# Three small moves inside the mixers of a hybrid decoder: a bank, a granule, and rows dealt 5 and 3

## The chip, the core and the metric

The kernel runs on one core of a Trainium2 chip. The metric is the device time of one execution in microseconds. Engines are named as in the profile: PE is TensorE (PEld its weight loads), DVE VectorE, ACT ScalarE, POOL GpSimd, SP SyncE, which issues most DMAs. Each engine works through its own list of instructions in order, and semaphores hold an instruction until what it needs is there.

## What is computed

Two decoder layers on x of 512 tokens by 1024 features, float32. Each layer is a half-step SwiGLU, three token mixers side by side, and a second half-step SwiGLU:

```
for l in range(2):
    x = x + 0.5 * swiglu(rms_norm(x, ffn1_norm[l]), ffn1_w_in[l], ffn1_w_out[l])
    h = rms_norm(x, mix_norm[l]) @ w_mix_in[l]
    c_x, c_b, c_c, h_q, h_f, h_i, h_g, f_q, f_k, f_v, f_f = split(h)
    y = concat(short_conv(c_x, c_b, c_c),        # 256 channels: rows 0 and 1 of 128
               hgrn2(h_q, h_f, h_i, h_g),        # 4 heads of 64: rows 2 and 3
               fox(f_q, f_k, f_v, f_f))          # 8 heads of 64: rows 4 to 7
    x = x + y @ w_mix_out[l]                     # 1024 x 1024
    x = x + 0.5 * swiglu(rms_norm(x, ffn2_norm[l]), ffn2_w_in[l], ffn2_w_out[l])
```

The convolution is causal, three taps wide, and gated before and after. HGRN2 is a linear recurrence with per-channel decay, done in chunks of 64 tokens. Fox is causal softmax attention with normalised q and k and a forget gate: the logit of query t and key s gets c[t] - c[s], where c is the running sum over tokens of the log of a sigmoid of the gate f_f.

## The kernel before

Activations lie transposed, features on the 128 partitions and tokens in the free dimension. For accuracy each float32 operand is split in a high and a low part (fp32r), and a product is three matmuls: high by high (L316), high by low (L322), low by high (L323), all in `mm3`. A 512-column matmul is the unit of the projections.

Weights come in **granules** (`granule`, L280): one or more DMAs on SP's queue bring up to two blocks of 128 rows into a staging buffer `st` (two buffers); an ACT cast (L305) writes the high part into a buffer `hl` (three buffers), and a DVE subtraction (L306) the low part. A granule of 256 columns in two row blocks feeds 12 matmuls of 512 columns into two banks. `stream_steps` (L331) yields after each granule, so that other work can be put in between.

PSUM has eight banks, which `bank` (L248) hands out under four names: `mm` three, `sc` two, `pt` two, `po` one. `sc` is used for attention scores and some of HGRN2, `pt` for transposes, `po` for the attention's output, `mm` for projections. A bank is free for the next taker of its name when the last reader of its previous content is through. `next4` (L251) takes either `sc`, `sc`, `pt`, `pt` or `mm`, `mm`, `mm`, `po`.

The code is a Python program that gives out instructions; the framework then orders each engine's list, by the order in which instructions are given out as a priority, and by when it reckons their operands and buffers ready. An instruction given out later can thus stand earlier on its engine, if the one before it is reckoned not ready.

The mixer (`mix`, L997) goes in this order:

1. Projections for HGRN2, values together with the fox gates (into `mm`, `sc`, `sc`, `mm`).
2. HGRN2 (`hgrn`, L1237), with the fox projections of q, k and v put between its steps. Beside its first two steps run the two parts of `fox_decay` (L1461): first the log of the gates, split in `flh` and `fll` (L1471, L1472); then their running sum over tokens, eight small matmuls against a triangle of ones (L1477) into one bank `cb` (L1474, a `pt` bank), from which ACT and DVE make `negc` (L1482, L1483). The step of HGRN2 given out just before transposes two blocks into the two `pt` banks (L1284), from which ACT copies them (L1287).
3. Attention, heads 0 to 3 (`fox_attend`, L1549). Each of 16 turns stands for one head and 128 queries: scores run three turns ahead (L1558, L1559 into `sc`), a softmax on DVE and ACT (L1563 to L1571), transposes of the probabilities P into `pt` (L1623), their split (L1625, L1626), and with each second turn the products with V (L1581 into `po`). After each head the two halves of the `po` bank are added (L1594, L1595), and after each second head the row of 128 features is split (L1598, L1599; tiles `fyh`, `fyl`). `beside` (L1158) puts the convolution's twelve granules (`conv`, L1145) between the turns, one per turn from n = 2 on, with n counted from `first`. At n = 3 the function `finish` gives out the rest of HGRN2, which reads two `pt` banks (L1442 and L1445).
4. Attention, heads 4 to 7, with most of the out-projection beside it (`most`, L1181): four groups of 256 output columns, each into two `mm` banks, each over the first rows of `order` (L1168). Rows 2 and 3 are HGRN2 (tile `hy`), 0 and 1 the convolution (`cyh`, `cyl`), 4 and 5 heads 0 to 3, 6 and 7 heads 4 to 7.
5. The remaining rows of the out-projection, in two groups of 512 columns, each into four banks of `next4`. Each bank is added to x (L1179), and the pieces of the next norm are made from it (`norm_part`). The second FFN follows.

Of the kernel before, what the change touches and what calls it, by code (L numbers as in the profile page):

```python
# [156 lines left out]
class Trunk:  # L157
# [109 lines left out]
    def act(self, out, in_, func, **kw):  # L267
        i = self.nc.scalar.activation(out, in_, func, **kw)
        if self.tab is not None:
            self.tc.add_manual_dep(i.ins, self.tab, NOSYNC, reason="table order")  # L270
        self.tab_users.append(i.ins.name)
        return i
# [724 lines left out]
    def mix(self, l, w, w_out, conv_w, out_gain, q_gain, k_gain, f_bias, next_gain):  # L997
# [3 lines left out]
        with tc.tile_pool(name=self.n("mix"), bufs=1) as mp:  # L1001
# [103 lines left out]
            def projections():  # L1105
                for hf in range(2):
                    yield from self.fox_qkv(mp, hf, tokens, half)

            dense = projections()
# [46 lines left out]
                    self.conv_out(ap2, i, bb[i])  # L1156

            def beside(attend, dense, first=0, then=()):  # L1158
                for n, _ in enumerate(attend, first):
                    if n == 3 and then:  # L1160
                        then()
                    if n >= 2:
                        next(dense, None)
                for _ in dense:
                    pass

            self.begin_norm(next_gain)
            order = [2, 3, 4, 5, 0, 1, 6, 7]  # L1168

            def rows(k0, a, n):  # L1170
                return lambda k, kk: [
                    w_out[order[k0 + k] * P : (order[k0 + k] + kk) * P, a : a + n]
                ]

            def act(k0):
                return lambda k: (self.yh[order[k0 + k]], self.yl[order[k0 + k]])

            def add(j, bank):
                nc.vector.tensor_add(self.xT[:, j, :], bank, self.xT[:, j, :])  # L1179

            def most():  # L1181
                for dg in range(4):
                    banks = [self.bank("mm") for _ in range(2)]
                    yield from self.stream_steps(
                        [(bk, c, None) for bk, c in zip(banks, FM2)],
                        rows(0, 256 * dg, 256), act(0), 6,
                    )
                    for i in range(2):
                        add(2 * dg + i, banks[i])

            beside(attend, conv(), 1, finish)
            beside(self.fox_attend(ap1, 1, half[1], qkg, {}), most())
            self.ntog = 0
            for dg in range(2):
                banks = self.next4()
                self.stream(
                    [(bk, c, None) for bk, c in zip(banks, TOK)],
                    rows(6, 512 * dg, 512), act(6), 2,
                )
                for i in range(4):  # L1200
                    j = 4 * dg + i
                    add(j, banks[i])
                    self.norm_part(j, ap2)
# [257 lines left out]
    def fox_decay(self, mp, zf):  # L1461
        nc = self.nc
        a = mp.tile([P, 4, NH], F32, tag="fa", name=self.n("fa"))
        lf = mp.tile([P, 4, NH], F32, tag="fl", name=self.n("fl"))
        nc.vector.scalar_tensor_tensor(out=a, in0=zf, scalar=-1.0, in1=zf, op0=ALU.mult, op1=ALU.min)
        self.act(a, a, AF.Exp)
        self.act(a, a, AF.Ln, bias=1.0)
        nc.vector.scalar_tensor_tensor(out=lf, in0=zf, scalar=0.0, in1=a, op0=ALU.min, op1=ALU.subtract)
        lh = mp.tile([P, 4, NH], F32R, tag="flh", name=self.n("flh"))
        ll = mp.tile([P, 4, NH], F32R, tag="fll", name=self.n("fll"))  # L1470
        nc.scalar.copy(lh, lf)  # L1471
        nc.vector.tensor_sub(ll, lf, lh)  # L1472
        yield
        cb = self.bank("pt")  # L1474
        for j in range(4):
            for part in (lh, ll):
                nc.tensor.matmul(  # L1477
                    cb[:NH, j * P :], part[:, j, :], self.utri[:, : T - j * P],
                    start=j == 0 and part is lh, stop=j == 3 and part is ll,
                )  # L1480
        self.negc = mp.tile([NH, 2, T], F32R, tag="negc", name=self.n("negc"))
        nc.scalar.activation(self.negc[:, 0, :], cb[:NH, :], AF.Copy, scale=-1.0)  # L1482
        nc.vector.scalar_tensor_tensor(  # L1483
            out=self.negc[:, 1, :], in0=cb[:NH, :], scalar=-1.0, in1=self.negc[:, 0, :],
            op0=ALU.mult, op1=ALU.subtract,
        )
# [338 lines left out]
```

## Time and profile before

| | us |
|---|---|
| median of 3 runs | 1816.66 (1815.56 to 1819.09) |
| the profiled execution | 1815.31 |
| its span, first to last instruction | 1813.2 |
| PE busy | 1801.3 (99%) |
| DVE busy | 1461.3 (81%) |
| ACT busy | 1001.0 (55%) |

One execution was profiled; its times are counted from its first instruction. The mixers lie at about 320 to 584 us and 1216 to 1480 us, the rest is FFNs. A line of a timeline has the start, the duration, engine, source line, operation, output and inputs by the program's names (buffer numbers left out), shapes and count; in brackets stands the time that the engine was idle before it, and what ended the wait. Matmuls overlap in a pipeline, so their rate is read from the distance of their starts, not from their duration. A line of the table of groups has, after the count, busy time and mean duration in ns, and then the idle time before them. A line of the table of stages has the stretch, its length, and busy time with the number of instructions for each engine.

### The profile page before, as it was taken

The numbers are of one execution on the slowest core, as the hardware profiler recorded it, in microseconds if no ns is written. First come the engines' busy times: TensorE is split into PE (matmuls) and PEld (weight loads), VectorE is DVE, ScalarE is ACT, GpSimd is POOL, SyncE is SP. The second block draws the span as 40 slices with busy tenths as digits, with TensorE's granted clock in tenths as the row PEclk, the third lists the DMA queues.
The fourth block names the chain that finished last, engine by engine and source line by source line (L and its number), as shares of the span: only waits on it lengthen the run. The fifth ranks groups of instructions, "written<-read, shape, count | busy, mean of one in ns | idle before, by whom it ended". The sixth has DMA issues, their size and how long they took to land.

```text
span 1813.2 us, 34777 instructions
## 1 busy us (share of the span) xinstructions
PE 1801.3 (99%) x14281; PEld 1682.8 (93%) x14281; DVE 1461.3 (81%) x2048; ACT 1001.0 (55%) x1434; POOL 170.3 (9%) x172
## 2 busy tenths in 40 slices
PE   9999999999999999999999999999999999999999
PEld 7899999899878899999889999998998788999997
DVE  9889787676887898889678887976868878888883
ACT  5455555464775565555445555555547755555551
POOL 0011120100000001112001111201000000020210
PEclk9999999999999999999999999999999999999999
DMA  6768783233323757868275787823233237687762
GB/s 197 186 135 191 179 175 96 74 79 85 87 82 105 216 136 161 197 159 168 82 207 130 163 193 192 163 68 79 77 90 86 82 102 212 163 158 192 158 134 93
DMA packets 243934, 250.94 MB, mean 138 GB/s; under 512 B 18456, under 2 KB 229152, under 8 KB 243776
## 3 DMA queue, kind: packets, MB, share of 16 engines
q1 hardware_dynamic: 189872, 182.38, 33.3%
q0 software_dynamic: 53600, 66.09, 22.8%
q8 instruction: 112, 1.84, 0.4%
q14 instruction: 46, 0.38, 0.1%
q10 hardware_dynamic: 304, 0.27, 0.0%
HBM read 223.98 MB, written 2.10 MB: 125 GB/s over the span
## 4 chain that ended last, share of the span: by engine, by line
PE 91%; DVE 5%; ACT 3%; issue 1%; DMA 0%; SPq 0%; ACTq 0%; DVEq 0%
PE mm L316 13%; PE mm L323 13%; PE mm L322 13%; PE sc L323 6%; PE sc L316 6%; PE sc L322 6%; PE pt L316 6%; PE pt L322 6%; PE pt L323 6%; PE po L316 4%; PE po L322 4%; PE po L323 4%; PE po L1581 1%; PE pt L1623 1%; ACT hl L305 1%
## 5 line engine op out<-in xcount | busy, mean ns | idle before, releaser
L784 ACT CAST hl<-w 128x1024 fp32r<-128x1024 f32 x322 | 337.1, 1049 | 318.2 <-PE mm L323 78.1
L786 DVE TENSOR_TENSOR hl<-w,hl 128x1024 fp32r<-128x1024 f32 x322 | 392.6, 1222 | 85.4 <-ACT hl L784 85.3
L306 DVE TENSOR_TENSOR hl<-st,hl 128x512 fp32r<-128x512 f32 (+2 forms) x188 | 161.6, 860 | 100.7 <-ACT hl L305 99.8
L305 ACT CAST hl<-st 128x512 fp32r<-128x512 f32 (+2 forms) x188 | 141.8, 754 | 176.8 <-PE po L323 62.3
L316 PE MATMUL mm<-xc,hl 128*128 128x256 f32 (+1 forms) x732 | 201.6, 276 | 0.5 <-ACT g L895 0.5
L323 PE MATMUL mm<-xc,hl 128*128 128x256 f32 x728 | 201.4, 277 | 0.0
L322 PE MATMUL mm<-xc,hl 128*128 128x256 f32 x728 | 201.4, 277 | 0.0
L323 PE MATMUL sc<-xc,hl 128*128 128x256 f32 x528 | 146.3, 277 | 0.0
L316 PE MATMUL sc<-xc,hl 128*128 128x256 f32 (+1 forms) x530 | 146.3, 277 | 0.0
L322 PE MATMUL sc<-xc,hl 128*128 128x256 f32 x528 | 146.2, 277 | 0.0
L316 PEld LDWEIGHTS mm<-xc,hl 128*128 128x128 f32 x732 | 137.4, 188 | 0.9 <-ACT g L895 0.7
L323 PEld LDWEIGHTS mm<-xc,hl 128*128 128x128 f32 x728 | 136.7, 188 | 0.1
L322 PEld LDWEIGHTS mm<-xc,hl 128*128 128x128 f32 x728 | 136.7, 188 | 0.0
L322 PE MATMUL pt<-xc,hl 128*128 128x256 f32 x480 | 133.0, 277 | 0.0
L316 PE MATMUL pt<-xc,hl 128*128 128x256 f32 (+1 forms) x484 | 133.0, 276 | 0.0
L323 PE MATMUL pt<-xc,hl 128*128 128x256 f32 x480 | 132.8, 277 | 0.0
L316 PE MATMUL mm<-x,hl 128*128 128x512 f32 x272 | 107.4, 395 | 0.0
L323 PE MATMUL mm<-x,hl 128*128 128x512 f32 x272 | 106.5, 392 | 0.4 <-DVE hl L306 0.4
L322 PE MATMUL mm<-x,hl 128*128 128x512 f32 x272 | 106.4, 391 | 0.0
L316 PEld LDWEIGHTS sc<-xc,hl 128*128 128x128 f32 x530 | 99.6, 188 | 0.2
L323 PEld LDWEIGHTS sc<-xc,hl 128*128 128x128 f32 x528 | 99.3, 188 | 0.1
L322 PEld LDWEIGHTS sc<-xc,hl 128*128 128x128 f32 x528 | 99.1, 188 | 0.0
(514 smaller groups left out, 5604.9 us busy)
## 6 DMA issues: line engine op xcount, KB each, us to landing
w<-in_ffn_w_in_dram SPq DMA_DIRECT2D x140, 512.0 KB
w<-in_ffn_w_out_dram SPq DMA_DIRECT2D x64, 512.0 KB
w<-in_ffn_w_out_dram POOLq DMA_DIRECT2D x56, 512.0 KB, 9.0
st<-in_w_mix_in_dram SPq DMA_DIRECT2D x88, 256.0 KB
st<-in_ffn_w_in_dram SPq DMA_DIRECT2D x70, 256.0 KB
w<-in_ffn_w_in_dram POOLq DMA_DIRECT2D x35, 512.0 KB, 8.2
w<-S POOLq DMA_DIRECT2D x35, 512.0 KB, 4.7
st<-in_ffn_w_out_dram SPq DMA_DIRECT2D x24, 512.0 KB
```

The source lines that it names most:

```text
L305: a = nc.scalar.copy(hi, src[:, c : c + w])
L306: b = nc.vector.tensor_sub(lo, src[:, c : c + w], hi)
L316: i = nc.tensor.matmul(acc[:, c], ah, bh[:, c], start=first and c.start == 0, stop=False, skip_group_check=True,)
L322: nc.tensor.matmul(acc, ah, bl, start=False, stop=False, skip_group_check=True)
L323: i = nc.tensor.matmul(acc, al, bh, start=False, stop=last, skip_group_check=True)
L784: A(nc.scalar.copy(hi, src))
L786: return lambda: V(nc.vector.tensor_sub(lo, src, hi))
L1581: nc.tensor.matmul(self.ob[:, t0 + u * P : t0 + 2 * P], V[:, j, h % 4].rearrange("p a d -> p (a d)"), part[:, j, u:, :].rearrange("p i t - ...
L1623: nc.tensor.transpose(tb[:, j * P : (j + 1) * P], p[:, j * P : (j + 1) * P], self.ident)
```

## The change

Three edits, none of which changes what is computed.

The fox gates' sums go into an `sc` bank instead of a `pt` bank. `beside` takes `first` granules of the dense work before the first turn that it drives; it is 1 for the convolution and 0 for the out-projection, so the convolution's granules each come one turn earlier. In the out-projection the rows' order becomes 2, 3, 0, 1, 4, 5, 6, 7, and five rows instead of six run beside the second half of the attention (granules of two, two and one row), which leaves three instead of two for the end (a granule of two rows, 5 and 6, and a granule of one row, 7, in each group).

```diff
             def beside(attend, dense, first=0, then=()):
+                for _ in range(first):
+                    next(dense, None)
                 for n, _ in enumerate(attend, first):
...
-            order = [2, 3, 4, 5, 0, 1, 6, 7]
+            order = [2, 3, 0, 1, 4, 5, 6, 7]
...
                         [(bk, c, None) for bk, c in zip(banks, FM2)],
-                        rows(0, 256 * dg, 256), act(0), 6,
+                        rows(0, 256 * dg, 256), act(0), 5,
...
                     [(bk, c, None) for bk, c in zip(banks, TOK)],
-                    rows(6, 512 * dg, 512), act(6), 2,
+                    rows(5, 512 * dg, 512), act(5), 3,
...
-        cb = self.bank("pt")
+        cb = self.bank("sc")
         for j in range(4):
```

## The prediction

> **What bounds the kernel now.** I read the page first, then busy time by stage, then the timeline of TensorE (PE) wherever two matmuls start further apart than their size needs.
>
> ```profile
> span 1813.2 us, 34777 instructions
> PE 1801.3 (99%) x14281; PEld 1682.8 (93%) x14281; DVE 1461.3 (81%) x2048; ACT 1001.0 (55%) x1434; POOL 170.3 (9%) x172
> PE 91%; DVE 5%; ACT 3%; issue 1%; DMA 0%; SPq 0%; ACTq 0%; DVEq 0%
> ```
>
> PE is the bound: 99% busy, 91% of the chain that ended last. No edit takes a matmul away, so the time can fall only by stalls of PE that vanish. By stage (columns: window, its length, then busy time of PE, PEld, DVE, ACT, POOL, then the granted clock):
>
> ```profile
> 470.00:518.00 48.00, 46.76 (x246) 38.23 (x246) 43.05 (x100) 36.75 (x83) 1.56 (x3) 1.00 0.29 78
> 518.00:566.00 48.00, 47.56 (x256) 38.32 (x255) 38.56 (x98) 35.08 (x81) 1.04 (x2) 1.00 0.32 91
> 566.00:584.00 18.00, 17.75 (x90) 14.03 (x89) 12.46 (x21) 9.83 (x18) 0.00 (x0) 1.00 0.26 83
> 584.00:1212.00 628.00, 628.00 (x4947) 605.27 (x4946) 521.80 (x577) 338.40 (x394) 75.84 (x64) 1.00 0.68 162
> 1364.00:1414.00 50.00, 48.83 (x257) 39.95 (x256) 43.61 (x101) 38.75 (x89) 2.08 (x4) 1.00 0.29 78
> ```
>
> The FFNs in the middle row idle 0.00 of 628 us. The attention half beside the convolution (first row) idles 1.24, the half beside the out-projection (second) 0.44, the mixer's tail (third) 0.25; the second layer's like half (last row) 1.17. The clock is 1.00 everywhere. So the stake is small: a few stalls per layer, each found twice.
>
> **Edit 1, the bank of the gates' sums.** Around L1477, from a timeline of all engines, then PE alone in layer 2:
>
> ```profile
> 388.32 0.19 DVE L1472 TENSOR_TENSOR fll<-fl,flh 128x32 fp32r<-128x32 f32 x1 [0.28 <-ACT flh L1471]
> 388.44 0.28 PE L322 MATMUL mm<-hl,x 128*128 128x256 f32 x1
> 388.56 0.28 PE L323 MATMUL mm<-hl,x 128*128 128x256 f32 x1
> 388.72 1.07 ACT L1287 COPY T<-pt 128x512 f32<-128x512 f32 x2
> 389.35 0.39 PE L1477 MATMUL pt<-utri,flh 128*8 128x512 f32 x1 [0.51 <-ACT T L1287]
> 391.72 0.67 DVE L1483 SCALAR_TENSOR_TENSOR negc<-pt,negc 8x512 fp32r<-8x512 f32 x1
> ```
> ```profile
> 1284.20 0.28 PE L323 MATMUL mm<-hl,x 128*128 128x256 f32 x1
> 1284.92 0.40 PE L1477 MATMUL pt<-utri,flh 128*8 128x512 f32 x1 [0.44 <-ACT T L1287]
> ```
>
> The last operand, `fll`, is ready at 388.51, but the sums start at 389.35, when the first of two ACT copies has emptied a `pt` bank. Matmuls of 256 columns start 0.12 apart (388.44, 388.56), so the gap of 0.79 holds 0.67 of stall; in layer 2 0.72 - 0.12 = 0.60. A `sc` bank has no such reader. The two of the value projection must have been read by v and zf before those inputs existed. The sums leave their bank at 391.72 + 0.67 = 392.39, and the next user of `sc`, L1318, starts only at 395.8:
>
> ```profile
> 395.78 0.34 PE L1318 MATMUL sc<-v,T 64*64 64x64 f32 x7
> ```
>
> So nothing else is late. The next thing the sums wait for is `fll`: if the sums are put right behind the transposes, PE waits for it from about 388.3 to 388.55. So the gain is 0.42 to 0.67; I take 0.5 per layer.
>
> **Edit 2, a granule ahead of the first turn of P.** PE, then DVE, then PE in layer 2:
>
> ```profile
> 468.20 0.40 PE L1558 MATMUL sc<-KA,QA 128*128 128x512 f32 x1
> 468.84 0.45 PE L316 MATMUL mm<-x,hl 128*128 128x512 f32 x1
> 471.18 0.39 PE L322 MATMUL mm<-x,hl 128*128 128x512 f32 x1
> 471.40 0.39 PE L323 MATMUL mm<-x,hl 128*128 128x512 f32 x1
> 472.82 0.33 PE L1623 MATMUL pt<-ident,P 128*128 128x128 f32 x1 [1.03 <-DVE T L1445]
> ```
> ```profile
> 470.41 0.68 DVE L306 TENSOR_TENSOR hl<-st,hl 128x512 fp32r<-128x512 f32 x1
> 472.07 0.69 DVE L1445 SCALAR_TENSOR_TENSOR T<-pt,T 128x512 f32<-128x512 f32 x1 [0.18 <-ACT T L268]
> 474.06 0.68 DVE L1563 CUSTOM_DVE_ANT_0 P<-sc,zm 128x512 f32<-128x512 f32 x1
> ```
> ```profile
> 1367.06 0.39 PE L323 MATMUL mm<-x,hl 128*128 128x512 f32 x1
> 1368.38 0.33 PE L1623 MATMUL pt<-ident,P 128*128 128x128 f32 x1 [0.94 <-DVE T L1445]
> ```
>
> A 512-column matmul takes its 0.22 to 0.23 (471.18, 471.40), so 1.42 holds a stall of 1.19; in layer 2 1.32 - 0.23 = 1.09. The turn waits for a `pt` bank that L1445 reads, and L1445 itself waited for an ACT square. But the granule that the edit puts ahead (468.84 to 471.40) **already stands ahead** of the turn: the code gives it out later, the schedule pulled it forward. Moving it in the code moves its two loads, its cast, its subtraction and its twelve matmuls in priority, past four score matmuls only (468.20 to 468.84); those become the cover of the last 0.64 us instead. L1445 comes no earlier, as the rest of HGRN2 is still issued at n = 3. What could fill the hole is the next granule, whose parts are ready at 470.41 + 0.68 = 471.09 and which now ranks one step higher, but still below the turn. Bounds: 1.19 gained if the schedule lets it pass; a loss of up to 0.64 if the delayed scores are missed. The scores' own reduction follows only at 474.06 in DVE's order, so I exclude most of that loss. I take 0.3 per layer, nearest to no change of order.
>
> **Edit 3, rows 5 and 3.** Counts: before 4 x 2 x 6 x 3 + 2 x 4 x 2 x 3 = 192 matmuls, after 4 x 2 x 5 x 3 + 2 x 4 x 3 x 3 = 192. Twenty-four matmuls, 24 x 0.225 = 5.4 us, go from beside the second half to the tail.
>
> What it removes: row 5 (heads 2 and 3) was wanted while it was being made.
>
> ```profile
> 524.34 0.46 PE L316 MATMUL mm<-hy,hl 128*128 128x512 f32 x1
> 524.82 0.74 PE L316 MATMUL mm<-fyh,hl 128*128 128x512 f32 x2
> 525.75 0.28 PE L1559 MATMUL sc<-KB,QB 66*128 66x256 f32 x1
> 526.22 0.50 PE L322 MATMUL mm<-fyl,hl 128*128 128x512 f32 x1 [0.20 <-DVE fyl L1599]
> ```
> ```profile
> 521.01 0.68 DVE L1234 TENSOR_TENSOR cyl<-cu,cyh 128x512 fp32r<-128x512 f32 x1
> ```
>
> Stalls: 0.48 - 0.23 = 0.25 and 0.47 - 0.12 = 0.35. The convolution's rows, which take that place, are ready at 521.69. Late next are the weights: a granule of one row covers 6 x 0.225 = 1.4 us instead of 2.7, with three `hl` buffers as before. So I book half, 0.3 per layer, with bounds 0.6 gained and 0.4 lost.
>
> What it does to the tail:
>
> ```profile
> 575.76 0.28 PE L1581 MATMUL po<-PL,V 128*128 128x128 f32 x1
> 576.85 0.39 PE L323 MATMUL mm<-fyh,hl 128*128 128x512 f32 x1
> 577.43 0.50 PE L316 MATMUL po<-fyh,hl 128*128 128x512 f32 x1 [0.19 <-DVE fo L1595]
> 578.23 0.40 PE L316 MATMUL sc<-fyh,hl 128*128 128x512 f32 x1
> ```
>
> Row 7 runs from 578.23. Before it PE does row 6 in seven banks; the eighth, `po`, is held by the last heads until L1595, which costs 0.58 - 0.23 = 0.35. Filler that needs neither `po` nor row 7 counts 144 + 7 x 3 = 165 matmuls before, 120 + 7 x 6 = 162 after: three fewer, 0.7 us. If the last heads end at the same place, the stall grows from 0.35 to 1.05; if they end earlier, because 24 matmuls less stand among them, it is gone. Queued behind it on PE is row 7, and behind that FFN2. Bounds +0.7 and -0.35; I take 0.
>
> **Casts.** Sixteen granules instead of fourteen, of the same columns:
>
> ```profile
> L306 DVE TENSOR_TENSOR hl<-st,hl 128x512 fp32r<-128x512 f32 x120 | 82.6, 689 | 48.6 <-ACT hl L305 47.9
> L305 ACT CAST hl<-st 128x512 fp32r<-128x512 f32 x120 | 73.9, 616 | 80.3 <-PE po L323 37.2 <-PE mm L323 34.8 <-DMA st<-in_w_mix_in_dram 7.9
> L306 DVE TENSOR_TENSOR hl<-st,hl 128x1024 fp32r<-128x1024 f32 x60 | 73.3, 1222 | 51.1 <-ACT hl L305 50.9
> L305 ACT CAST hl<-st 128x1024 fp32r<-128x1024 f32 x60 | 62.9, 1048 | 90.7 <-PE pt L323 29.9 <-PE po L323 25.1 <-DMA st<-in_ffn_w_out_dram 11.0
> ```
>
> Two lines through these sizes leave 2 x 616 - 1048 = 184 ns per cast and 2 x 689 - 1222 = 156 ns per subtraction that do not shrink: 0.4 and 0.3 us more per layer, in the tail, where DVE is busy 12.46 of 18 us. Hidden: 0. The Trainium skill, Perfetto Trace Analysis, section Optimizing Scalar/DVE Operations, speaks against such splitting: each operation has a fixed overhead, and larger ones help if the engine is saturated. By that rule the sum would be 0.6 us worse over both layers; by the tail's row DVE has room.
>
> **The sum.** Per layer -0.5 - 0.3 - 0.3 + 0 = -1.1, so -2.2. The profiled execution took 1815.31 (span 1813.2 and 2.1 around it); it would take 1813.1. The median shown is 1816.66, 1.35 above it; I forecast **1814.5**.
>
> **Rivals.**
> (A) All stalls go: per layer 0.6 + 1.1 + 0.6 + 0.35 = 2.7, together -5.3: 1811.4. For it: each has a named cause that an edit touches. Against: the turn's order looks unchanged.
> (B) Slower: the second half is paced by DVE's chain per turn, not by PE. Without the 24 matmuls it holds 48 - 5.4 = 42.6 us of PE work beside 38.56 - 4 x 0.26 = 37.5 of DVE (a 256-column subtraction is 0.43 on the line above, 0.26 less). If DVE gets no denser than its 80% now, the half lasts 37.5 / 0.803 = 46.7, PE idles up to 4.1 more, and the 24 matmuls still come in the tail. It decides against the change once a layer idles over 1.1 us more; seven tenths of the price, 2.9, give 2 x (2.9 - 1.1) = +3.6: 1820.3. For it: DVE's chain already delays PE in the first half. Against: there DVE reached 43.05 of 48.
> (C) Nothing: the bank's gain is eaten by the tail, where `po` and the three `hl` buffers now serve four granules and FFN2's first cast waits for one of them: -0.5 + 0.7 per layer, +0.4: 1817.1. The Trainium skill, same page, section Optimization Strategy, reads gaps that repeat as too few buffers. Against this: FFN2's row of before idles 0.00.
>
> **How the numbers follow.** Forecast 0.42, A 0.25, B 0.18, C 0.15. A measurement tells about 0.2%, 3.6 us, from no change. Forecast and C lie within it; A beyond it; a few hundredths of the forecast too: faster 0.28, same 0.54, slower 0.18. The forecast's own range is 1812.5 to 1816.5; the range given reaches from just below A, 1811.2, into B, 1820.0, and leaves out the far ends of both.
>
> **What would show it.** L1477 starting within 0.3 us of the matmul before it; L1623's first wait still about 1 us (forecast) or gone (A); no wait on L1599 near 525; the wait before the first `po` matmul of the tail between 0 and 1.05; PE idle in the second half near 0.4 (forecast) or above 2 (B). Wrong would make it a schedule that falls out differently at places no edit names.

## The result, and the profile after

| | before | after |
|---|---|---|
| median, 22 runs each, us | 1816.81 (1814.47 to 1823.05) | 1812.72 (1810.13 to 1817.63) |
| after / before | | 0.9977, 95% interval 0.9969 to 0.9984 |
| the profiled execution, us | 1815.31 | 1817.26 |
| its span, us | 1813.2 | 1815.5 |

The change gains 4.1 us by the medians (0.23%, interval 2.9 to 5.6). The execution of after that was profiled is one of its slower ones: its span is longer than that of before although its mixers are shorter. The last section shows where that comes from: from the FFNs, whose matmuls the edits leave as they were. So the traces are compared by pieces, not by spans.

The page of after: span, busy time of PE, shares of the chain that ended last.

```profile
span 1815.5 us, 34793 instructions
...
PE 1804.4 (99%) x14281; PEld 1689.7 (93%) x14281; DVE 1458.4 (80%) x2052; ACT 1001.2 (55%) x1438; POOL 170.3 (9%) x172
...
PE 91%; DVE 4%; ACT 3%; issue 1%; DMA 0%; SPq 0%; ACTq 0%; DVEq 0%
```

PE has the same 14281 matmuls; DVE and ACT have four instructions more each, the casts and subtractions of the four additional granules. Busy time by stage in after, columns as before; the mixer now ends at 583 instead of 584:

```profile
470.00:518.00 48.00, 46.73 (x250) 38.95 (x249) 42.63 (x100) 36.12 (x82) 2.09 (x4) 1.00 0.29 78
518.00:566.00 48.00, 46.98 (x260) 38.36 (x259) 40.88 (x106) 39.15 (x91) 1.04 (x2) 1.00 0.30 88
566.00:583.00 17.00, 17.00 (x83) 13.91 (x82) 12.55 (x20) 8.97 (x14) 0.00 (x0) 1.00 0.30 94
```

The tail idles 0.00 instead of 0.25. The half beside the convolution idles 1.27, as before; the half beside the out-projection 1.02 instead of 0.44. Read alone, the second row would say that the change lost something there. Two things mislead. The work has moved against the window, which now takes in the wait ahead of the last head's first product with V (565.34, below); before, that place lay in the next window, at 571.06. And idle time counts only the part of a stall that outlasts the matmul records before it, which last 0.39 and start 0.23 apart: in before the matmul at 571.06 starts 0.45 behind the one ahead of it, 0.23 more than usual, and no idle time is shown for it; in after the same place shows 0.41. **Idle time in windows with fixed borders misleads once the work has shifted**; from here on the pieces run from one matmul to another.

A layer's mixer from its first matmul to FFN2's first, in before and then in after:

```profile
339.65 0.39 PE L316 MATMUL mm<-x,hl 128*128 128x512 f32 x1
...
583.72 0.39 PE L316 MATMUL sc<-x,hl 128*128 128x512 f32 x1
```
```profile
340.59 0.39 PE L316 MATMUL mm<-x,hl 128*128 128x512 f32 x1
...
582.93 0.39 PE L316 MATMUL sc<-x,hl 128*128 128x512 f32 x1
```

That is 244.07 before and 242.35 after (the rows are rounded), and in layer 2 243.79 and 242.19: 1.66 per layer on average, 3.3 in all, inside the interval of the medians. By places the 1.7 of layer 1 split in three: 0.70 before the first state matmul of HGRN2 (L1318 before), 0.53 between the first turn and the last product with V, 0.49 in the tail. For the last two, whose matmuls the deal moved, I took **lost time**: the distance from one start to the next above the median distance for a matmul of that size in before, summed over the piece. It falls from 4.34 to 4.08 between the first matmul on HGRN2's rows and the last product with V, where the second row showed more idle time. (Lines from L1158 on stand two higher in after: L1477 is L1479, L1623 L1625, L1445 L1447.)

**The bank.** After, from a timeline of all engines:

```profile
388.15 1.04 PE L1286 MATMUL pt<-ident,T 128*128 128x128 f32 x8
...
388.77 0.22 ACT L1473 CAST flh<-fl 128x32 fp32r<-128x32 f32 x1 [0.26 <-DVE fl L1470]
...
389.02 0.19 DVE L1474 TENSOR_TENSOR fll<-fl,flh 128x32 fp32r<-128x32 f32 x1 [0.28 <-ACT flh L1473]
389.04 0.40 PE L1479 MATMUL sc<-utri,flh 128*8 128x512 f32 x1
...
389.28 0.40 PE L1479 MATMUL sc<-utri,fll 128*8 128x512 f32 x1
```

The sums start right behind the eight transposes, with no wait (no bracket).

**The first turn.** PE in after, in layer 1 and layer 2, then DVE:

```profile
471.29 0.39 PE L1560 MATMUL sc<-KA,QA 128*128 128x512 f32 x1
...
471.81 0.28 PE L1561 MATMUL sc<-KB,QB 66*128 66x128 f32 x1
473.05 0.33 PE L1625 MATMUL pt<-ident,P 128*128 128x128 f32 x1 [0.96 <-DVE T L1447]
```
```profile
1367.38 0.33 PE L1625 MATMUL pt<-ident,P 128*128 128x128 f32 x1 [1.00 <-DVE T L1447]
```
```profile
472.31 0.69 DVE L1447 SCALAR_TENSOR_TENSOR T<-pt,T 128x512 f32<-128x512 f32 x1 [0.18 <-ACT T L268]
```

The granule now stands ahead of the four score matmuls, which are the last cover, and the wait of about 1 us is still there.

**Row 5 and the tail.** PE in after, where the second half begins and where the mixer ends:

```profile
525.14 0.40 PE L322 MATMUL mm<-cyl,hl 128*128 128x512 f32 x1
525.38 0.22 PE L1560 MATMUL sc<-KA,QA 128*128 128x128 f32 x1
...
526.59 0.40 PE L323 MATMUL mm<-fyh,hl 128*128 128x512 f32 x1
527.30 0.44 PE L1560 MATMUL sc<-KA,QA 128*128 128x384 f32 x1 [0.32 <-DVE nm L1565]
...
564.53 0.40 PE L316 MATMUL sc<-fyh,hl 128*128 128x512 f32 x1
565.34 0.39 PE L1583 MATMUL po<-PH,V 128*128 128x256 f32 x1 [0.41 <-ACT PH L1627]
...
570.24 0.28 PE L1583 MATMUL po<-PL,V 128*128 128x128 f32 x1
...
576.59 0.39 PE L323 MATMUL mm<-fyh,hl 128*128 128x512 f32 x1
576.81 0.39 PE L316 MATMUL po<-fyh,hl 128*128 128x512 f32 x1
```

No matmul waits for `fyh` or `fyl` near 525 any more; a wait for a softmax (0.71 between starts at 526.59, 0.71 - 0.23 = 0.48 of it stall; 0.54 in layer 2) has come nearby. In the tail the first `po` matmul follows 0.22 behind the one before it, without the 0.35 of before. The last head waits once for its probabilities, 0.81 - 0.23 = 0.58.

### The profile page after: what moved, and what is told of

Read it like the earlier page. It is cut to its first block, busy times and chain, and to the rows that moved or that the text cites. A ratio compares the mean times of both kernels' runs of the same rounds, so it can differ in the third digit from the quotient of the medians.

```text
span 1815.5 us, 34793 instructions
## 1 busy us (share of the span) xinstructions
PE 1804.4 (99%) x14281; PEld 1689.7 (93%) x14281; DVE 1458.4 (80%) x2052; ACT 1001.2 (55%) x1438; POOL 170.3 (9%) x172
## 4 chain that ended last, share of the span: by engine, by line
PE 91%; DVE 4%; ACT 3%; issue 1%; DMA 0%; SPq 0%; ACTq 0%; DVEq 0%
PE mm L316 13%; PE mm L323 13%; PE mm L322 13%; PE sc L323 7%; PE sc L322 6%; PE sc L316 6%; PE pt L316 6%; PE pt L322 6%; PE pt L323 6%; PE po L316 4%; PE po L323 4%; PE po L322 4%; PE po L1583 1%; DVE hl L306 1%; PE pt L1625 1%
## 5 line engine op out<-in xcount | busy, mean ns | idle before, releaser
L306 DVE TENSOR_TENSOR hl<-st,hl 128x512 fp32r<-128x512 f32 (+3 forms) x192 | 162.1, 844 | 104.2 <-ACT hl L305 103.3
L305 ACT CAST hl<-st 128x512 fp32r<-128x512 f32 (+3 forms) x192 | 142.6, 743 | 175.3 <-PE po L323 67.4
```

The source lines that it names most:

```text
L305: a = nc.scalar.copy(hi, src[:, c : c + w])
L306: b = nc.vector.tensor_sub(lo, src[:, c : c + w], hi)
```

## The experiments

The theory to be tested: PE sets the time, each edit takes away PE's stalls at its own place, and the three gains add. Against it stood that a stall that vanishes comes back at the next late operand, so that the edits' gains are not those of their places.

Totals scatter by several us from run to run, so 1 us per layer is not to be had from a few of them. The length of a layer, taken as above from each kernel's trace, repeats much better: the changed kernel, profiled a second time, gives 242.28 and 242.11. The two layers of one kernel are two samples; they lie up to 0.8 apart, in ten of the fourteen profiles less than 0.5. So a difference of 0.3 between two means says little by itself. Lost time by pieces repeats better: that of the second half, from the first matmul on HGRN2's rows to the last product with V, agrees within 0.1 between the layers in every kernel but e_deal. All kernels:

```
kernel       layer 1  layer 2   mean   against before
before        244.07   243.79  243.93
after         242.35   242.19  242.27   -1.66
after_again   242.28   242.11  242.20   -1.73
e_bank        243.59   243.20  243.40   -0.53
e_granule     243.49   243.17  243.33   -0.60
e_order       243.39   243.46  243.43   -0.50
e_deal        244.41   243.63  244.02   +0.09
gd            242.83   242.69  242.76   -1.17
d44           243.07   242.81  242.94   -0.99
two           242.61   241.97  242.29   -1.64
late          243.86   243.41  243.64   -0.29
after_late    242.71   242.44  242.58   -1.35
f_n1          244.15   243.41  243.78   -0.15
f_first       242.70   241.95  242.33   -1.60
```

Five of them ran only once, with totals of 1816.88 (after_again), 1813.46 (gd), 1815.06 (d44), 1818.03 (late) and 1812.80 (after_late); they are used for their traces alone.

**Each edit alone.** From before, the bank alone (e_bank), the granule alone (e_granule), the order of the rows alone with six and two rows as before (e_order), and the order with five and three rows (e_deal):

```diff
e_bank:     cb = self.bank("pt")  ->  cb = self.bank("sc")
e_granule:  + for _ in range(first): next(dense, None)
e_order:    order = [2, 3, 4, 5, 0, 1, 6, 7]  ->  [2, 3, 0, 1, 4, 5, 6, 7]
e_deal:     e_order, and act(0), 6 -> 5; rows(6 ...), act(6), 2 -> rows(5 ...), act(5), 3
```

> Edit 1 alone. Theory S (the gain is the sum of stalls of PE that each edit takes, and they add): the sums start right behind the transposes, the stretch from the mixer's first matmul to the first one of L1318 is 0.7 us shorter in each layer, everything behind it is as before, and the time falls by 1.4 us (ratio 0.9992). Rival L (a new schedule falls out differently at places that no edit names): the 0.7 is given back further on, or more than 2 us are gained.

> Edit 2 alone. Theory S: the granule already stood ahead of the first turn, so the turn still waits 1.0 to 1.2 us for its bank, with the four score matmuls now between granule and turn; 0 to 0.3 us per layer are gained in the rest of the first half, 0 to 0.6 us in all. Rival: the wait goes, 1.1 us per layer, 2.2 us in all.

> The rows' order of edit 3 alone, still dealt 6 and 2. Theory S: the two waits for row 5 near the first group (0.6 us per layer) go, or come back smaller when row 5 is used as third granule; the wait before the first po matmul of the tail stays at about 0.35 us; 0.3 to 0.6 us per layer, 0.6 to 1.2 us in all. Rival T (the deal, not the order, brings what edit 3 brings, by more filler in the tail): no change.

> Edit 3 alone, order and deal 5 and 3. Theory S: the stretch of the out-projection and the tail lose 0.7 us of stalls per layer, 0.3 ahead of the last product with V and 0.5 behind it, 1.5 us in all; the wait before the first po matmul of the tail is gone. Rival B of the prediction (the second half paced by DVE): the second half idles 1 us or more longer and the time rises. Rival L: the share differs from that in the full change by more than 0.5 us per layer.

Totals: e_bank 1817.72 (ratio 1.0000, 0.9985 to 1.0014), e_granule 1815.78 (0.9992, 0.9977 to 1.0007), e_order 1818.73 (0.9997, 0.9983 to 1.0010), e_deal 1817.61 (0.9999, 0.9986 to 1.0012). No total tells any of them from before. By the layers the bank gives 0.53, all of it ahead of L1318 (56.13 to 55.58 and 55.90 to 55.21), the granule 0.60, the order 0.50. The deal with its order gives 0.16 in layer 2 and loses 0.34 in layer 1: it ends the wait ahead of the first `po` matmul (behind the last product with V 0.13 is lost instead of 0.58) and opens new ones in the second half, which loses 5.0 and 4.7 instead of 4.3. The largest, in layer 1, is at the first scores. PE in e_order, then in e_deal the ACT operation that makes the keys and PE in layer 1 and layer 2, then the first turn in e_granule and its row 5:

```profile
526.45 0.40 PE L316 MATMUL mm<-fyh,hl 128*128 128x512 f32 x1
527.46 0.45 PE L1558 MATMUL sc<-KA,QA 128*128 128x384 f32 x1 [0.61 <-DVE nm L1563]
```
```profile
522.20 0.69 ACT L1536 ACTIVATE KA<-pt,qkg 64x512 fp32r<-64x512 f32 x1
```
```profile
525.01 0.40 PE L316 MATMUL mm<-cyh,hl 128*128 128x512 f32 x1
526.49 0.30 PE L1558 MATMUL sc<-KA,QA 128*128 128x128 f32 x1 [1.08 <-DMA KA<-KA]
...
1424.68 0.28 PE L1558 MATMUL sc<-KA,QA 128*128 128x128 f32 x1
```
```profile
472.95 0.33 PE L1625 MATMUL pt<-ident,P 128*128 128x128 f32 x1 [0.93 <-DVE T L1447]
...
527.10 0.50 PE L322 MATMUL mm<-fyl,hl 128*128 128x512 f32 x1
```

In e_order the two waits for row 5 are gone, but a wait for a softmax stands in their place, 1.01 - 0.23 = 0.78 of stall against the 0.60 of before. So its 0.50 is not won where edit 3 looked for it: it comes 5 to 15 us later, where in layer 1 three waits of 0.2 to 0.3 between 531 and 540 become one of 0.24. The tail's wait stays (0.58 of lost time), as expected.

In e_deal the keys `KA`, half of which a DMA copies from the other half, land after PE asks for them: 1.48 between starts, 1.25 of stall. In layer 2 that wait is absent, and a softmax costs 0.68 instead. In e_granule the first turn waits as before, and the 0.60 come later: the waits for row 5 fall from 0.60 to 0.29 (`fyl` only), waits of 0.3 for `KB` come in near 488 and 539, and what is won beyond these is spread over gaps of less than 0.2.

**The granule and the deal together** (gd: the change without the bank).

> Edits 2 and 3 together, the sums back in a pt bank. The single edits shorten a layer's mixer, from its first matmul to the FFN's, by 0.53 (bank), 0.60 (granule) and -0.09 us (deal), 1.04 together, the full change by 1.66. Theory I (the deal needs the granule: alone it opens a wait of 1.1 us for the KA copy at the second half's first scores, which the earlier end of the convolution covers): no wait for that copy, 1.1 us shorter per layer. Rival A (the bank is what the others need; the two alone just add): the wait is there, 0.5 us shorter.

The two give 1.17, where alone they gave 0.60 and -0.09, as theory I had it. PE in gd, at the second half's first scores:

```profile
525.56 0.40 PE L322 MATMUL mm<-cyl,hl 128*128 128x512 f32 x1
525.80 0.22 PE L1560 MATMUL sc<-KA,QA 128*128 128x128 f32 x1
```

No wait for `KA` here. But theory I's reason, that the granule gives the copy its cover, is not borne out by the traces. In layer 1 of e_deal the scores start 3.60 us behind the end of the ACT operation that makes the keys (522.89 to 526.49); in its layer 2 they start 2.35 behind it without a wait (1422.33 to 1424.68), and in gd 2.54 (523.26 to 525.80). In layer 1 of e_deal PE was done with the matmul ahead at about 2.35, too, so gd asks for the keys hardly later. The copy took longer that once, in one layer of one kernel, and why stays open. In layer 2, free of that wait, the granule and the deal give 0.62 and 0.16 alone and 1.10 together: they still don't add, but 0.3 is over and not 0.7, and where that 0.3 comes from was not shown.

Put on one after the other the edits give 0.60 (granule), 0.57 (order and deal), 0.49 (bank). One kernel is missing: granule, bank and order with six and two rows as before. Alone these three give 0.60, 0.53 and 0.50, 1.63 together, which is as much as the whole change. So no run shows that dealing 5 and 3, rather than the order alone, adds anything to the sum, though the tail's wait went only where it was done.

**Other sizes of the same edits.** Two granules ahead of the first turn (two), and a deal of four and four (d44), both from after:

```diff
two:  beside(attend, conv(), 1, finish)  ->  beside(attend, conv(), 2, finish), with n counted from 2
d44:  act(0), 5 -> 4; rows(5 ...), act(5), 3 -> rows(4 ...), act(4), 4
```

> The full change with two granules of the convolution ahead of the first turn instead of one. Theory H (the turn waits 1.1 us for HGRN2's last readers of the bank whatever stands ahead of it, and a second granule fills that time): the wait at the first turn under 0.3 us, the mixer 0.5 to 1.1 us shorter per layer than with the full change, 1 to 2 us in all. Rival K (a turn that comes 1.6 us later delays the softmax chain behind it): the wait goes but comes back within the first half, no gain.

> The full change with the rows dealt 4 and 4 instead of 5 and 3. Theory F (the tail's wait is gone with 5 and 3 already, so a longer tail has nothing left to win, and thinner filler among the turns lets PE wait): the mixer 0.3 to 1 us longer per layer than with the full change. Rival (more filler for the end is still better): 0.2 us shorter or more.

PE in two, at its first turn and in the second half, and PE in d44:

```profile
474.61 0.39 PE L1561 MATMUL sc<-KB,QB 66*128 66x512 f32 x1
474.85 0.27 PE L1625 MATMUL pt<-ident,P 128*128 128x128 f32 x1
...
541.17 0.40 PE L322 MATMUL mm<-hy,hl 128*128 128x512 f32 x1
541.68 0.41 PE L1625 MATMUL pt<-ident,P 128*128 128x128 f32 x2
```
```profile
553.15 0.30 PE L1625 MATMUL pt<-ident,P 128*128 128x128 f32 x1
554.18 0.30 PE L1560 MATMUL sc<-KA,QA 128*128 128x128 f32 x1 [0.73 <-DMA KA<-KA]
```

In two the first turn's wait is gone in both layers (1.1 each), and the layer is no shorter: 242.29 against 242.27 (total 1815.24, ratio 0.9986, 0.9970 to 1.0002). What was gained comes back in the second half, where the lost time between the first matmul on HGRN2's row and the last product with V grows from 4.1 to 5.4: 0.4 and 0.6 in stalls of 0.2 to 0.6 (a new one of 0.51 - 0.23 = 0.28 is in the rows above), the rest in eight more gaps of about 0.1. In d44 the tail gains nothing further, since there is no wait left in it, and the second half pays 0.7 for the missing cover, in layer 1 by the wait for `KA` first, in layer 2 by waits for a softmax and for a cast: 5 and 3 is better than 4 and 4.

**Where the granule's gain comes from.** Not at the first turn, that much was plain. With the granule ahead the convolution ends one granule earlier (174.4 to 174.8 us into the layer instead of 176.3 to 176.5, by the last matmul on its weights). Two kernels give one granule more at n = 9, far from the first turn, from before (late) and from after (after_late):

```diff
                     if n >= 2:
                         next(dense, None)
+                    if first and n == 9:
+                        next(dense, None)
```

> The kernel before with edit 2 put elsewhere: not a granule of the convolution ahead of the first turn, but a second granule in the turn n = 9, so that the convolution ends one granule earlier and the first turns stay as they were. The granule ahead of the first turn, alone, shortened a layer by 0.6 us (243.9 to 243.3), although the first turn's wait of about 1 us stayed; of that, 0.3 came between the first turn and the first matmul on HGRN2's rows, 0.3 between that and the last product with V. Theory E (the gain is that the convolution ends one granule earlier, so that the out-projection's granules and their casts come earlier): this kernel gains the same, a layer of 243.2 to 243.5, in the same two stretches. Rival G (the gain is the changed order around the first turns, where scores stand after the granule): a layer of 243.8 to 244.0, as before, or longer if two granules in one turn starve for one of the two staging buffers (a wait on a DMA or a cast of 0.5 us or more near the turn n = 9).

> The changed kernel with one further granule of the convolution, in the turn n = 9, so that the convolution ends two granules earlier than before the change. Two granules ahead of the first turn took the first turn's wait away (1.1 us a layer) but gave back 1.3 us in the second half, for a layer of 242.3, the same as the changed kernel's 242.27. Theory E2 (what was given back is the price of a convolution that ends two granules early, since the out-projection then runs dry of cover in the later turns): here the first turn's wait stays and the second half gives back about as much, a layer of 242.9 to 243.6. Rival G2 (what was given back belongs to the new order of the first turns): the second half stays at the changed kernel's loss of 4.1 us, a layer of 242.3 or less.

PE in late, where keys come late, and in after_late:

```profile
526.18 0.30 PE L1560 MATMUL sc<-KA,QA 128*128 128x128 f32 x1 [0.32 <-DMA KA<-KA]
...
539.00 0.41 PE L1625 MATMUL pt<-ident,P 128*128 128x128 f32 x2 [0.42 <-DVE KB L1545]
```
```profile
521.43 0.66 PE L1627 MATMUL pt<-ident,P 128*128 128x128 f32 x4 [0.26 <-ACT P L1573]
...
529.01 0.45 PE L1562 MATMUL sc<-KA,QA 128*128 128x384 f32 x1 [0.42 <-DVE nm L1567]
```

Late gains 0.29, half of what the granule ahead gained: the 0.3 between the first HGRN2 row and the last product with V are there, the 0.3 before it are not (0.05). The two stretches are alike in both layers, so this stands although the means are 0.3 apart. Half of the gain thus comes with the earlier end of the convolution (theory E). The other half needs more than that: the place ahead of the first turn (G), or the granules of the turns before n = 9, which late leaves where they were; these two were not told apart.

After_late loses 0.31 against after, and lies between its two theories. Its first turn waits as before; between that and HGRN2's rows it loses 0.9 instead of 1.4, and in the second half 4.9 instead of 4.1. It doesn't price two exactly, as its expectation assumed: as n counts from 2 there, the convolution of two ends two turns ahead of that of after (170.0 to 170.6 us into the layer against 173.9 to 174.1), that of after_late one (172.5 to 172.8). The second half pays 0.8 for the first of these turns and, unless the new order ahead of the first turn has a share in it, 1.3 for both. So one granule early gains, and in this kernel a second one costs more than it brings.

**Why the first turn still waits.** The prediction's reason was that the vector operation that frees its bank (L1447 after) is given out at n = 3. Two kernels give the rest of HGRN2 out earlier, at n = 1 (f_n1) and ahead of the granule (f_first), else as after:

```diff
f_n1:     if n == 3 and then:  ->  if n == 1 and then:
f_first:  beside(attend, conv(), 1, finish)  ->  finish(); beside(attend, conv(), 1)
```

> The changed kernel with the rest of HGRN2 (the function finish, which holds the vector operation that frees the bank for which the first turn waits 1.1 us per layer) given out at n = 1 instead of n = 3, two turns earlier in priority; nothing else differs. Theory P (the first turn's wait is a matter of priority: the rest of HGRN2 is given out behind the granule and the first turns, so its chain comes late): the wait shrinks to below 0.5 us and the layer by 0.6 or more, 242.27 to 241.7 or less, unless it is given back. Rival D (the chain is bound by its own operations on ACT and DVE, since the two sums over channels stand just before it, and the schedule already starts each as soon as its input is there): the wait stays within 0.2 of 1.1 us and the layer within 0.2 of 242.27. A third way, K2 (the vector engine is the scarce one in this half: the operations pulled forward delay the first softmax): the first turn's wait goes, and waits of as much on the softmax or on the split of a granule's weights come later in the same half, a layer of 242.1 to 242.8.

> The changed kernel with the rest of HGRN2 given out ahead of the granule and of the first turn, the earliest place that it can have after the two sums over channels. Theory P: the first turn's wait is gone, a layer of 241.2 to 241.7. Rival D: the wait stays at about 1.1 us, a layer of 242.1 to 242.5. K2: the wait goes and comes back later in the half, a layer of 242.1 to 242.8 or, where the softmax is held up at the start, up to 243.3.

ACT in after and in f_first, with PE's turn in f_first, then PE in f_n1:

```profile
467.75 1.05 ACT L268 ACTIVATE T<-T 128x1024 f32<-128x1024 f32 x1
...
469.99 0.61 ACT L305 CAST hl<-st 128x512 fp32r<-128x512 f32 x1
470.49 0.47 ACT L1519 ACTIVATE V<-mm,invc 128x256 fp32r<-128x256 f32 x1
470.86 0.47 ACT L1519 ACTIVATE V<-po,invc 128x256 fp32r<-128x256 f32 x1
471.22 1.06 ACT L268 ACTIVATE T<-T 128x1024 f32<-128x1024 f32 x1
```
```profile
471.19 1.05 ACT L268 ACTIVATE T<-T 128x1024 f32<-128x1024 f32 x1
```
```profile
473.02 0.33 PE L1626 MATMUL pt<-ident,P 128*128 128x128 f32 x1 [0.97 <-DVE T L1448]
```
```profile
472.68 0.33 PE L1625 MATMUL pt<-ident,P 128*128 128x128 f32 x1 [0.98 <-DVE T L1447]
...
489.85 0.30 PE L1560 MATMUL sc<-KA,QA 128*128 128x128 f32 x1 [1.33 <-ACT hl L305]
```

Rival D holds for the wait: it is 0.9 to 1.0 in both, as in after. The chain is an exponential on ACT (467.75), its square (471.22), L1447 behind the square (472.31), the turn (473.05). The exponential has ended at 468.80, and the square starts 2.4 us later, behind scalings and another exponential of P, a cast and two copies of V, at the same place of ACT's list wherever the code gives it out. So place in the code doesn't move it. That the turn would come earlier with the square further up in ACT's list follows from the chain, but no run here changed that order. f_n1 pays 1.3 to 1.5 per layer at a second place, near 488, for a cast or a DMA that comes late; f_first is as after by its layers. Its median, 1811.36 (ratio 0.9963, 0.9948 to 0.9977; f_n1: 1813.21, 0.9990, 0.9975 to 1.0006), is the lowest of all, but the interval overlaps that of after, and the mixers show no gain: not shown to be better.

## Why the prediction was right, and where not

The forecast of 1814.5 (own range 1812.5 to 1816.5) is met by 1812.72 at its lower edge. The direction and the bound were right; the gain was 1.66 per layer instead of 1.1, and 3.3 of the 4.1 by the medians is found in the mixers. By places in layer 1, the bank brought 0.70 for the 0.5 booked, the stretch from the first turn to the last product with V 0.53 for 0.6, and the tail 0.49 for 0. That the middle term fits is luck: it was not won at the places named.

- **What bounds the kernel**: right. The count of matmuls and the clock of 1.00 are unchanged, and everything won is stall of PE.
- **Edit 1, 0.5 forecast**: 0.7 at its place, 0.49 to 0.53 in the layer's length. The upper bound of 0.67 held, within what a stretch varies; the lower one, 0.42, let PE wait for `fll`, but the first sum reads `flh` alone (ready 388.99), and `fll` is needed only 0.24 later. Nothing else in `sc` was late, as argued.
- **Edit 2, 0.3 forecast**: 0.60 alone. Its account of the first turn was right in both halves: the granule already stood ahead, and the wait stays (1.12 and 1.16 of stall after, 1.19 and 1.09 before). The failed step is to have looked for the gain there. The convolution's twelve granules all move up a turn, and the end of that chain, 50 us later, was not priced; about half of the 0.60 comes with it (late). The reason given for the wait (n = 3) was also wrong: f_first gives the operations out first, and the wait is 0.97.
- **Edit 3, 0.3 at row 5 and 0 in the tail**: the waits on `fyh` and `fyl` went, and 0.48 of stall at a softmax came, so the place itself gave about 0.1, and with the order alone it lost 0.2; "late next are the weights" named the wrong successor, it was the softmax in after and e_order, and the keys in layer 1 of e_deal. The tail gave 0.49, all that was lost there but 0.1: of the bounds +0.7 and -0.35 the lower one was right. The branch that held is the one with the last heads ending earlier: the last product with V stands 576.81 - 570.24 = 6.6 us ahead of the first `po` matmul, instead of 577.43 - 575.76 = 1.7, so `po` is free in time. The casts cost nothing: the tail's row idles 0.00.
- **Rival A** (all stalls go, 1811.4): half of it. The bank's and the tail's stalls went, the first turn's didn't. **Rival B** (the second half paced by DVE): DVE is the releaser of the new wait, but PE idles 1.02 in that window and the layer is shorter, so the turning point was not reached; d44, with fewer rows still, loses 0.7, but its largest waits are for a DMA (layer 1) and a cast on ACT (layer 2). **Rival C** named `po` and the three `hl` buffers, and beside it the rule of the Trainium skill, Perfetto Trace Analysis, Optimization Strategy, that gaps that repeat can mean too few buffers; in after the first `po` matmul of the tail shows no wait, so the rule decided nothing here.

So what the sum lacked is the tail, booked at 0 and worth 0.49 per layer, and 0.2 at the bank.

## What to carry over

Moving a chain of filler work by one step changes every place where the chain's end meets other work: price the end of the chain, not only the place of the edit. A stall that an edit takes away pays only if the next operand in line (here a softmax, keys by DMA, a cast) is early by as much: the two waits for row 5 made way for a softmax, and in two a vanished wait of 1.1 gave nothing. Before a wait is made the reason for something, look for it in the other layer: the largest one of e_deal stood in one of the two. Where totals scatter by more than the effect, measure from matmul to matmul in the trace: one kernel's layers repeated within 0.1 us here, totals within several.

## What was not expected of the hardware

The FFNs have the same matmuls in all kernels and no idle time, and yet differ in length. Before, then after, by windows (first number behind the window's length: busy time of PE and its matmuls; 1.00 is the granted clock):

```profile
1580.00:1620.00 40.00, 40.00 (x356) 40.00 (x355) 34.49 (x36) 20.01 (x24) 8.06 (x7) 1.00 0.73 155
```
```profile
1580.00:1620.00 40.00, 40.00 (x342) 40.00 (x341) 33.98 (x36) 20.16 (x23) 8.45 (x8) 1.00 0.72 146
```

A matmul of 256 columns starts every 113 ns in the one and every 117 to 118 ns in the other, with the weight loads as dense and the clock the same. In after this holds for some 120 us: from the second layer's FFN2 to the last matmul it takes 334.25 us, where before took 329.70. That, and not the mixers, is why its profiled span is longer. The second profile of after has it at the same place (342 in this window); e_granule has it there too, and at 1000 to 1100 (851 matmuls against 885 of before). Over the fourteen profiles this last part, from FFN2 on, takes 333.3 to 334.3 us in seven (both of after among them) and 329.6 to 330.6 in the other seven: before, e_bank, gd, two, late, after_late and f_first. Kernels close to after are on both sides. Only after was profiled twice, so it isn't shown whether the slower pace belongs to an execution or to a kernel, nor why it comes; but a stretch of this size is worth more than the whole change.
